# When the products of a state-space step are issued: the steps' waits are split in halves

## The chip, the cores and the metric

The kernel runs on one core of one Trainium2 chip. The metric is the device time of one execution in microseconds (us). Engines are called as in the profile: PE (TensorE, matrix products), PEld (its weight loads), DVE (VectorE), ACT (ScalarE), POOL (GpSimd), SP (SyncE, which here starts DMAs).

## The reference

Two layers of a hybrid backbone on 256 context tokens and 256 latent tokens, width 2048, in float32. Each layer normalizes and modulates the tokens, multiplies them by one large input weight, feeds three mixers side by side (a gated linear recurrence "LRU" in both directions, windowed attention, and a state-space mixer "SSD" in both directions), and multiplies their outputs by one large output weight. The part around the change is the chunked state-space sum:

```python
    Acs = jnp.cumsum(dt * A.reshape(G, R), axis=2)
    ...
    decay = jnp.exp(jnp.where(tril, seg, -jnp.inf))
    CB = jnp.einsum('bcign,bcjgn->bcijg', Cm, Bm)
    Wm = CB[..., None] * decay * dt[:, :, None]
    y_diag = jnp.einsum('bcijgr,bcjgrp->bcigrp', Wm, x)
    w_state = jnp.exp(A_last[:, :, None] - Acs) * dt
    states = jnp.einsum('bcjgn,bcjgrp->bcgrpn', Bm, x * w_state[..., None])
    ...
    y_off = jnp.einsum('bcign,bcgrpn->bcigrp', Cm, h_in) * jnp.exp(Acs)[..., None]
    y = (y_diag + y_off).reshape(bsz, L, SSD_HEADS, SSD_HEAD_DIM)
```

The sequence is cut into chunks of 128 tokens: a state per chunk, carried from chunk to chunk, and for each chunk an output from the tokens within it (`y_diag`) and from the carried state (`y_off`).

## The kernel before

The large weights go through PE in blocks of 128x128, 16 for one column tile of the input weight. A DMA brings four blocks (`raw`), ACT copies them to the rounded format (`hi`, L237), DVE subtracts to get the rest (`lo`, L238), and PE multiplies each block in three passes (hi by u, hi by the rest of u, lo by u; all through the helper's L174, as `acc<-u,hi` and `acc<-u,lo`). Three passes are called a block below. A block is 512 columns wide in layer 0, and partly 256 in layer 1, where some columns are needed for the latent tokens alone.

Between blocks the mixers' own work is issued. Each mixer is a Python generator that yields a wait; the kernel keeps a planned clock (`self.clock`) that only PE's instructions move forward, a full block by 0.647 (three times 512/2400+0.0025), and after each block `pump()` resumes those generators whose wait is over. So a wait is a number of blocks, rounded up, and PE's order is fixed in the program by these waits. The orders of DVE, ACT, POOL and SP are made from it by the language's scheduler, by its own model. None of the planned times is a measured one.

`ssd_core` is one of these generators. It goes through 28 steps in layer 0 and 20 in layer 1. A step has a beginning, its elementwise work, and an end, its products:

- State: the beginning is one DVE multiplication (`xw`, L1119). The end is the PE product `mx<-xw,Btok`, then ACT copies it to `H` (L1128), or DVE multiplies `H` by its decay (L1130) and adds the product (L1132).
- Output, written y(chunk, half) below: the beginning is, for the first half of a chunk, the PE product `mx<-CT,BT` and two masks of it (`cbm`, L1151); for each half two DMAs of broadcast rows (`bc`, L1158, four buffers) and the decays: `ee` in four columns on ACT (L1164) and DVE (L1165), `ww` in four columns on ACT (L1167) and DVE (L1168), an exponential (L1170), `ee` times `ww` (L1171), and for each carried state an exponential of `bc` (L1175) and a multiplication by CT (L1176). The end is 12 small PE products (`mx<-ee,X`, `mx<-bc,H`), or 8 where only one state is carried, and one DVE addition (L1191). The first group's chunk order is 0, 1, 3, 2, the second's too.

The LRU runs at the same time. For each of its columns it issues two "gate pairs", one per direction, a short wait ("lx2") apart: four products `mx<-xc,gw` and `mx<-xsw,gw` into two buffers, each freed by a tanh on ACT (`lt`, L712). Further ACT work (L717, L718, L720, and a square root with its table load at L724), POOL (L727) and DVE scans (L730, L733, L735) follow. State products, `mx<-CT,BT`, output products and gate pairs take turns in four PSUM buffers `mx`; three more, `acc`, hold the large products.

`self.wait("core")` is 4 in layer 0 and 5.2 in layer 1. The waits differ in blocks: 4 is 7 full blocks, 5.2 is 9 full blocks or 16 of half width. Work that waits for `core_done`: the z column tiles of a layer, which follow later in the program, and in layer 0 `ada_wide` (DMA at L377, DVE at L380), which computes later modulations.

Of the kernel before, what the change touches and what calls it, by code (L numbers as in the profile page):

```python
# [139 lines left out]
class Kernel:  # L140
# [471 lines left out]
    def ssd_core(self, l):  # L612


        yield lambda: self.ssd_ready == 13
        ends = []
        for g in range(2):
            f1, r1 = self.ssd_state(0, g, 0), self.ssd_state(1, g, 1)
            steps = [f1, r1]
            if l == 0:  # L620
                steps += [self.ssd_y(g, 0, hh, None, r1) for hh in range(2)]
                steps += [self.ssd_y(g, 1, hh, f1, None) for hh in range(2)]
            f2, r2 = self.ssd_state(0, g, 1, f1, True), self.ssd_state(1, g, 0, r1, True)
            f3, r3 = self.ssd_state(0, g, 2, f2), self.ssd_state(1, g, 3, r2, True)
            steps += [f2, r2, f3]
            steps += [self.ssd_y(g, 3, hh, f3, r2) for hh in range(2)]
            steps += [r3]
            steps += [self.ssd_y(g, 2, hh, f2, r3) for hh in range(2)]
            for step in steps:
                step.begin()  # L630
                ends.append(step)
                yield self.wait("core")
                if len(ends) > 1:
                    ends.pop(0).end()
        yield self.wait("core")
        ends.pop(0).end()
        self.core_done = True

# [638 lines left out]
```

## Time and profile before

| what | before |
|---|---|
| median of 3 executions | 1833.83 us (1833.53 to 1835.87) |
| the profiled execution | 1829.47 us |
| its span | 1827.5 us |
| mean granted clock of PE | 0.991 |
| PE busy | 1765.5 us, 97% of the span |
| DVE busy | 1407.4 us, 77% |
| ACT busy | 973.3 us, 53% |

A busy share is a mean over the whole span. The steps of `ssd_core` run from about 257 to 453 us in layer 0 and from about 1265 to 1445 us in layer 1. Windows of the profile give the busy time of each engine within such a stretch. "PEclk" is the granted clock of PE, 1.00 for full speed. The list of PE's waits says for which operation's end PE stood idle, and the timeline shows such an idle time in brackets behind the instruction that ended it.

### The profile page before, as it was taken

The numbers are of one execution on the slowest core, as the hardware profiler recorded it, in microseconds if no ns is written. First come the engines' busy times: TensorE is split into PE (matmuls) and PEld (weight loads), VectorE is DVE, ScalarE is ACT, GpSimd is POOL, SyncE is SP. The second block draws the span as 40 slices with busy tenths as digits, with TensorE's granted clock in tenths as the row PEclk, the third lists the DMA queues.
The fourth block names the chain that finished last, engine by engine and source line by source line (L and its number), as shares of the span: only waits on it lengthen the run. The fifth ranks groups of instructions, "written<-read, shape, count | busy, mean of one in ns | idle before, by whom it ended". The sixth has DMA issues, their size and how long they took to land.

```text
span 1827.5 us, 30170 instructions
## 1 busy us (share of the span) xinstructions
PE 1765.5 (97%) x10522; PEld 1453.4 (80%) x10522; DVE 1407.4 (77%) x3117; ACT 973.3 (53%) x1798; POOL 214.7 (12%) x179
## 2 busy tenths in 40 slices
PE   7999999999999999999999999999989999999999
PEld 4677876667778778887888887888767788999999
DVE  4447769898899778899999536877688785788665
ACT  4324578688523354556232235545688863678443
POOL 0000111111210021211000021010021130121000
PEclk9999999999999999999999999999999999999999
DMA  9982333434675545556766433455243564554655
GB/s 364 389 292 66 124 104 102 122 122 146 220 221 180 179 150 185 178 182 221 238 220 222 158 122 107 133 185 168 96 138 107 179 214 142 182 178 155 217 185 179
DMA packets 186344, 322.99 MB, mean 177 GB/s; under 512 B 19121, under 2 KB 44625, under 8 KB 185553
## 3 DMA queue, kind: packets, MB, share of 16 engines
q1 hardware_dynamic: 186192, 321.09, 54.2%
q8 instruction: 82, 1.34, 0.3%
q14 instruction: 70, 0.57, 0.1%
HBM read 310.38 MB, written 10.63 MB: 176 GB/s over the span
## 4 chain that ended last, share of the span: by engine, by line
PE 72%; DVE 9%; issue 7%; ACT 7%; DMA 3%; POOL 1%; SPq 0%; ACTq 0%; DVEq 0%; POOLq 0%
PE acc L174 55%; PE mx L174 13%; PE ada L174 3%; DVE lo L238 2%; PE mx L170 2%; DMA bc<-acsD 1%; ACT hi L237 1%; DVE ada L380 1%; DVE araw L380 1%; ACT lt L712 1%; DVE lh L730 1%; DMA araw<-in_adaw_dram 1%; DVE xc L466 1%; DVE ee L1165 1%; ACT ww L1167 1%
## 5 line engine op out<-in xcount | busy, mean ns | idle before, releaser
L174 PE MATMUL acc<-u,hi 128*128 128x512 f32 (+1 forms) x4800 | 1277.4, 355 | 3.9 <-ACT u L452 3.1
L174 PEld LDWEIGHTS acc<-u,hi 128*128 128x128 f32 x4800 | 837.1, 190 | 149.0 <-issue 32.6
L174 PE MATMUL acc<-u,lo 128*128 128x512 f32 (+1 forms) x2400 | 842.4, 351 | 6.9 <-DVE lo L238 6.7
L237 ACT ACTIVATE hi<-raw 128x512 fp32r<-128x512 f32 x640 | 397.8, 628 | 544.4 <-PE acc L174 420.8
L238 DVE TENSOR_TENSOR lo<-raw,hi 128x512 fp32r<-128x512 f32 x640 | 457.9, 718 | 184.6 <-ACT hi L237 172.7
L174 PEld LDWEIGHTS acc<-u,lo 128*128 128x128 f32 x2400 | 455.5, 190 | 71.9 <-DVE lo L238 11.7
L380 DVE SCALAR_TENSOR_TENSOR araw<-araw,adac 128x512 f32<-128x512 f32 x256 | 183.2, 716 | 6.9 <-DMA araw<-in_adaw_dram 4.1
L380 DVE SCALAR_TENSOR_TENSOR ada<-araw,adac 128x512 f32<-128x512 f32 x192 | 141.6, 738 | 13.0 <-DMA adac<-condD 7.0
L174 PE MATMUL mx<-u,hi 128*128 128x512 f32 (+1 forms) x320 | 99.7, 395 | 0.0
L1077 DVE SCALAR_TENSOR_TENSOR X<-acc,mod,X 128x256 f32<-128x256 f32 x144 | 65.0, 478 | 39.5 <-PE acc L174 39.4
L727 POOL TENSOR_TENSOR lt<-lt,ltl 128x512 f32<-128x512 f32 x32 | 45.5, 1443 | 326.2 <-ACT ltl L724 305.3
L868 POOL TENSOR_SCALAR prob<-prob,qrs 128x512 f32<-128x512 f32 (+1 forms) x48 | 58.2, 1227 | 214.7 <-ACT hi L237 124.7
L427 POOL TENSOR_TENSOR ssq<-ssq,sq 128x512 f32<-128x512 f32 (+1 forms) x26 | 34.1, 1312 | 308.0 <-ACT sq L423 308.0
L174 PEld LDWEIGHTS mx<-u,hi 128*128 128x128 f32 x320 | 56.6, 191 | 14.2 <-issue 4.6
L174 PE MATMUL mx<-u,lo 128*128 128x512 f32 (+1 forms) x160 | 61.0, 382 | 0.0
L511 POOL TENSOR_SCALAR X<-xs,prm 128x512 f32<-128x512 f32 (+1 forms) x16 | 15.4, 968 | 361.6 <-DVE xs L489 357.1
L174 PE MATMUL mx<-xc,gw 64*64 64x512 f32 x128 | 40.8, 619 | 8.9 <-ACT lt L712 5.9
L423 ACT ACTIVATE sq<-X 128x256 f32<-128x256 f32 (+1 forms) x44 | 18.8, 452 | 54.8 <-DVE X L654 53.1
L1165 DVE SCALAR_TENSOR_TENSOR ee<-bc,nacs,ee 128x128 f32<-128x128 f32 x96 | 35.9, 427 | 15.0 <-DMA bc<-acsD 9.6
L771 POOL TENSOR_TENSOR qw<-qw,cst 128x256 f32<-128x256 f32 x20 | 23.1, 1156 | 197.7 <-DVE rt L770 169.7
L712 ACT ACTIVATE lt<-mx,gbh 128x512 f32<-128x512 f32 x64 | 42.0, 674 | 4.1 <-PE mx L174 4.0
L1164 ACT ACTIVATE ee<-bc,nacs 128x128 f32<-128x128 f32 x96 | 30.9, 390 | 17.7 <-DMA bc<-acsD 17.7
(240 smaller groups left out, 1953.1 us busy)
## 6 DMA issues: line engine op xcount, KB each, us to landing
raw<-in_w_in_dram SPq DMA_DIRECT2D x448, 256.0 KB, 2.8
araw<-in_adaw_dram SPq DMA_DIRECT2D x256, 256.0 KB, 3.0
raw<-in_w_out_dram SPq DMA_DIRECT2D x192, 256.0 KB, 3.0
ar<-in_ada_dram SPq DMA_DIRECT2D x84, 256.0 KB, 5.4
bc<-acsD SPq DMA_DIRECT2D x48, 256.0 KB, 3.7
ar<-in_ada_dram SPq DMA_DIRECT2D x22, 512.0 KB, 6.9
adac<-condD SPq DMA_DIRECT2D x28, 256.0 KB, 4.5
gw<-in_gates_dram SPq DMA_DIRECT2D x16, 256.0 KB, 2.9
```

Of the source, the lines that this page charges most:

```text
L170: self.nc.tensor.transpose(out=out, in_=lhsT, identity=rhs)
L174: self.nc.tensor.matmul(out=out, lhsT=lhsT, rhs=rhs, start=start, stop=stop, **kw)
L237: nc.scalar.activation(out=hi, in_=part, func=AF.Copy)
L238: nc.vector.tensor_tensor(out=lo, in0=part, in1=hi.bitcast(F32), op=ALU.subtract)
L380: i = nc.vector.scalar_tensor_tensor(out=o, in0=raw, scalar=1.0, in1=row[c].rearrange("p t x -> p (t x)"), op0=ALU.mult, op1=ALU.mult, acc ...
L427: nc.gpsimd.tensor_tensor(out=self.ssq[0], in0=self.ssq[0], in1=sq, op=ALU.add)
L712: nc.scalar.activation(out=t, in_=pg[g], func=AF.Tanh, scale=0.5, bias=self.gb[:, 16 * g + 8 * d + m:16 * g + 8 * d + m + 1])
L727: nc.gpsimd.tensor_tensor(out=ti, in0=ti, in1=tl[:, d], op=ALU.mult)
L868: nc.gpsimd.tensor_scalar(out=pr[j], in0=pr[j], scalar1=rs[:, j:j + 1], scalar2=1.0, op0=ALU.mult, op1=ALU.mult)
L1077: nc.vector.scalar_tensor_tensor(out=x[:, s], in0=acc[:, s.start - w0:s.stop - w0], scalar=mod[:, 2 * KT + m, c:c + 1], in1=x[:, s], op0=A ...
L1164: nc.scalar.activation(out=e[:, j], in_=bcs[0][:, j], func=AF.Identity, bias=k.nacs[:, f:f + 1])
L1165: nc.vector.scalar_tensor_tensor(out=e[:, j], in0=bcs[1][:, j], scalar=k.nacs[:, r:r + 1], in1=e[:, j], op0=ALU.add, op1=ALU.min)
```

## The change

The wait of a step is yielded in two halves, and the end of the step before is issued between them, where it stood behind the whole wait. The wait behind the last step is halved too. No instruction is added or removed; lines behind the change are one higher.

```diff
             for step in steps:
                 step.begin()
                 ends.append(step)
-                yield self.wait("core")
+                yield self.wait("core") / 2
                 if len(ends) > 1:
                     ends.pop(0).end()
-        yield self.wait("core")
+                yield self.wait("core") / 2
+        yield self.wait("core") / 2
         ends.pop(0).end()
         self.core_done = True
```

In planned blocks of layer 0, one step now follows the next by 8 blocks, where it was 7: each half of 2 is 4 blocks of 0.647, rounded up. A product stood two waits, 14 blocks, behind its step's beginning; now it stands three halves, 12 blocks, behind it. Counted from the start of the program, the first product of the core stands at block 248 (it was 250), the last at 440 (it was 422), and the z tiles begin at 448 in both. In layer 1, where most blocks are of half width, a wait of 5.2 and two of 2.6 are 16 blocks alike, and a product stands closer to its beginning by 2.6 of the planned clock. The pieces below are places where the order changed.

On DVE, in the same layer, where the elementwise work of y(1,0) of the first group ends. Before:

```order
L1165 SCALAR_TENSOR_TENSOR ee_2891<-bc_2889,nacs_2356,ee_2891 128x128 x4
L721 SCALAR_TENSOR_TENSOR ltl_2809<-la_594_2844,ltl_2809 128x512
L1168 SCALAR_TENSOR_TENSOR ww_2892<-cbm_2885,dt_2151,ww_2892 128x128 x4
L1168 SCALAR_TENSOR_TENSOR ww_2955<-cbm_2885,dt_2151,ww_2955 128x128 x4
L1176 TENSOR_TENSOR bc_2887<-bc_2887,CT_1802 128x512
L238 TENSOR_TENSOR lo_3038<-raw_3035,hi_3037 128x512
L1191 TENSOR_TENSOR X_1805<-mx_2940,X_1805 128x2x128
L1171 TENSOR_TENSOR ee_2891<-ee_2891,ww_2892 128x512
```

And now (`lh_595` is the LRU's forward scan):

```order
L1166 SCALAR_TENSOR_TENSOR ee_2900<-bc_2898,nacs_2356,ee_2900 128x128 x4
L722 SCALAR_TENSOR_TENSOR ltl_2783<-la_594_2844,ltl_2783 128x512
...
L1177 TENSOR_TENSOR bc_2896<-bc_2896,CT_1802 128x512
L238 TENSOR_TENSOR lo_3036<-raw_3033,hi_3035 128x512
L1169 SCALAR_TENSOR_TENSOR ww_2901<-cbm_2894,dt_2151,ww_2901 128x128 x4
L1192 TENSOR_TENSOR X_1805<-mx_2940,X_1805 128x2x128
L731 SCALAR_TENSOR_TENSOR lh_595_2850<-lt_583_2790,lt_584_2792 128x512
L1131 TENSOR_TENSOR H_2768<-H_2768,dec_2358 128x512
L1169 SCALAR_TENSOR_TENSOR ww_2973<-cbm_2894,dt_2151,ww_2973 128x128
L1172 TENSOR_TENSOR ee_2900<-ee_2900,ww_2901 128x512
```

The last operation that y(1,0) needs (L1171, now L1172) stands behind the LRU's forward scan; it stood ahead of it. On ACT the four `ww` of this step have also moved behind the LRU's table load and square root.

On PE, where the LRU's two gate pairs of one column meet the core's state products (in the first group, after the output run y(1,0), y(1,1)). Before, one state product and the first gate pair, two blocks, and the second gate pair:

```order
L174 MATMUL mx_3114<-xw_3030,Btok_1803 128x512
L174 MATMUL mx_3121<-xc_2994,gw_2653 64x512
L174 MATMUL mx_3122<-xc_2994,gw_2653 64x512
...
L174 MATMUL mx_3143<-xc_2994,gw_2653 64x512
L174 MATMUL mx_3144<-xc_2994,gw_2653 64x512
```

Now, the first gate pair, the state product right behind it, one block, and the second gate pair:

```order
L174 MATMUL mx_3118<-xc_2994,gw_2653 64x512
L174 MATMUL mx_3119<-xc_2994,gw_2653 64x512
...
L174 MATMUL mx_3134<-xw_3051,Btok_1803 128x512
L174 MATMUL acc_3104<-u_467,hi_3107 128x512
...
L174 MATMUL mx_3141<-xc_2994,gw_2653 64x512
L174 MATMUL mx_3142<-xc_2994,gw_2653 64x512
```

Five uses of the four `mx` buffers lie close together in both, but the two pairs are one block apart where they were two.

On PE again, at the last gate pairs that meet a state and an output's beginning together (second group, about block 386). Before, a state product, `mx<-CT,BT`, a gate pair, two blocks, and the second gate pair:

```order
L174 MATMUL mx_4102<-xw_4024,Btok_1803 128x512
L174 MATMUL mx_4106<-CT_1802,BT_1801 128x128
L174 MATMUL mx_4141<-xc_3988,gw_3637 64x512
L174 MATMUL mx_4142<-xc_3988,gw_3637 64x512
...
L174 MATMUL mx_4163<-xc_3988,gw_3637 64x512
L174 MATMUL mx_4164<-xc_3988,gw_3637 64x512
```

Now a gate pair, two blocks, the second gate pair and a state product right behind it:

```order
L174 MATMUL mx_4098<-xc_3950,gw_3621 64x512
L174 MATMUL mx_4099<-xc_3950,gw_3621 64x512
...
L174 MATMUL mx_4122<-xc_3950,gw_3621 64x512
L174 MATMUL mx_4123<-xc_3950,gw_3621 64x512
...
L174 MATMUL mx_4149<-xw_4051,Btok_1803 128x512
```

Six buffers were asked for within two blocks there, and now it is five, with the state product last.

## Rows read from the trace of the kernel before

**Rows 1.** The page: busy time, share of the span, instructions.
```profile
PE 1765.5 (97%) x10522; PEld 1453.4 (80%) x10522; DVE 1407.4 (77%) x3117; ACT 973.3 (53%) x1798; POOL 214.7 (12%) x179
```
**Rows 2.** PE's waits: what ended them; us in total, times, longest.
```profile
PE mx L174 <- ACT lt L712: 12.7, 8, 4.1
...
PE acc L174 <- DVE lo L238: 6.7, 9, 1.6
PE mx L174 <- DVE ee L1171: 4.5, 2, 3.1
...
PE mx L174 <- DVE H L1132: 2.7, 1, 2.7
PE mx L174 <- ACT xsw L694: 2.3, 1, 2.3
...
PE mx L174 <- ACT H L1128: 0.7, 2, 0.4
```
**Rows 3.** Windows: us; PE, PEld, DVE, ACT, POOL busy; PEclk; DMA share; GB/s.
```profile
257.00:453.00 196.00, 182.61 (x980) 130.44 (x979) 170.23 (x345) 154.66 (x306) 30.45 (x22) 0.97 0.37 117
290.00:300.00 10.00, 6.86 (x30) 5.50 (x30) 10.00 (x18) 5.94 (x16) 2.55 (x2) 0.66 0.32 112
339.00:347.00 8.00, 7.17 (x42) 4.71 (x42) 6.12 (x12) 8.00 (x15) 0.00 (x0) 0.79 0.33 98
440.00:450.00 10.00, 8.87 (x49) 5.87 (x50) 9.62 (x30) 9.71 (x18) 0.00 (x0) 0.83 0.48 155
453.00:580.00 127.00, 124.94 (x560) 99.59 (x560) 117.25 (x253) 51.38 (x82) 21.23 (x14) 1.00 0.66 214
1265.00:1445.00 180.00, 170.25 (x1030) 129.44 (x1029) 144.64 (x262) 137.61 (x246) 28.75 (x25) 0.99 0.38 122
```
**Rows 4.** Timeline of PE, layer 0: start, us, instruction, idle time before it.
```profile
293.20 0.70 PE L174 MATMUL mx<-ee,X 128*64 128x128 f32 x4 [3.15 <-DVE ee L1171]
...
339.83 0.77 PE L174 MATMUL mx<-xc,gw 64*64 64x512 f32 x1 [3.06 <-ACT lt L712]
...
371.73 0.40 PE L174 MATMUL mx<-ee,X 128*64 128x128 f32 x2 [1.33 <-DVE ee L1171]
372.53 0.32 PE L174 MATMUL mx<-bc,H 128*64 128x128 f32 x1 [0.39 <-ACT H L1128]
...
410.05 0.65 PE L174 MATMUL mx<-xc,gw 64*64 64x512 f32 x2 [2.75 <-DVE H L1132]
...
441.06 1.76 PE L174 MATMUL mx<-xsw,gw 64*64 64x512 f32 x4 [2.35 <-ACT xsw L694]
```
**Rows 5.** The chain of waits: 66 blocks of full width in one piece.
```profile
849.20 44.89 PE acc L174 x198
```
**Rows 6.** Timeline around y(1,0) and y(1,1), first group, ACT, DVE and PE.
```profile
280.92 1.28 ACT L724 ACT_TABLE_LOAD   x1
...
281.44 0.68 DVE L1171 TENSOR_TENSOR ee<-ee,ww 128x512 f32<-128x512 f32 x1
...
282.21 1.15 ACT L724 ACTIVATE ltl<-ltl,epss 128x1024 f32<-128x1024 f32 x1
...
283.89 0.45 PE L174 MATMUL mx<-ee,X 128*64 128x128 f32 x4
...
286.76 1.21 DVE L730 TENSOR_TENSOR_SCAN lh<-lt,lt 128x512 f32<-128x512 f32 x1
...
292.38 0.67 DVE L1171 TENSOR_TENSOR ee<-ee,ww 128x512 f32<-128x512 f32 x1
```
**Rows 7.** Timeline of PE, layer 1, the longest wait there.
```profile
1344.11 2.07 PE L174 MATMUL mx<-xw,Btok 128*128 128x512 f32 x2 [4.12 <-ACT lt L712]
```
**Rows 8.** Timeline of DVE and PE, layer 1, the output that starts soonest.
```profile
1432.29 0.68 DVE L1176 TENSOR_TENSOR bc<-bc,CT 128x512 f32<-128x512 f32 x1
...
1433.82 0.43 PE L174 MATMUL mx<-ee,X 128*64 128x128 f32 x2
```
**Rows 9.** The tile ada: durations min/median/max in ns, first and last start.
```profile
L380 DVE SCALAR_TENSOR_TENSOR ada<-araw,adac x192: 668/692/1795, 452.9 to 1016.6; 128x512 f32<-128x512 f32 x192
```

## The prediction

> **What bounds the kernel now.** The page comes first: PE is busy for 1765.5 us, 97% of the span [rows 1], so time can only be won or lost where PE stands idle or runs slowly. The windows show where the changed steps lie. From 257 to 453 us, the core of layer 0, PE is busy for 182.61 of 196.00 us, so 13.4 us are idle, and its mean granted clock is 0.97; right behind it, 453 to 580, it is busy for 124.94 of 127.00 at 1.00 [rows 3]. The core of layer 1, 1265 to 1445, has 9.75 us idle at a clock of 0.99. DVE is the busiest neighbour in layer 0, 170.23 of 196.00 (87%); ACT has 154.66. The list of PE's waits names the releasers: the tanh that frees the LRU's `mx` buffers 12.7 us in 8 waits, the last operation of an output's `ee` 4.5 us in 2, `H` 2.7 and 0.7, `xsw` 2.3 [rows 2]. The timeline gives the places in layer 0: 3.15 us before y(1,1) of the first group, 3.06 before a gate pair, 1.33 and 0.39 before y(0,0) of the second group, 2.75 before a gate pair that waits for `H`, 2.35 inside a gate pair [rows 4]. These sum to 13.03, nearly all of the window's idle time. Other waits, such as those for `lo`, are spread over the program and the change doesn't touch them.
>
> An idle stretch can cost twice. In 290 to 300 us the granted clock was 0.66, in 339 to 347 it was 0.79, in 440 to 450 it was 0.83 [rows 3], and each holds one of the long waits. The loss is 10 x 0.34 = 3.4, 8 x 0.21 = 1.7 and 10 x 0.17 = 1.7 us. Over the whole window it is 196 x 0.03 = 5.9 (rounded in the clock's second digit), so no other stretch is left, and the waits of 2.75 and 1.33 cost nothing more than themselves. The ceiling of any gain here is all of it: 13.4 + 5.9 + 9.75 + 180 x 0.01 = 30.9 us.
>
> **The change part by part.** No instruction is added or removed. A block takes 44.89 / 66 = 0.680 us [rows 5]. In layer 0 two things happen at once: steps follow each other after 8 blocks instead of 7, so the same DVE and ACT work is spread over a longer stretch, and a product stands 12 blocks behind its beginning instead of 14, so it is 2 x 0.680 = 1.36 us closer. The words for the change (later) fit the begins, not this distance.
>
> *First output run.* Before, y(1,0) had slack: its last DVE operation ran from 281.44 for 0.68 and its products began at 283.89, so 1.77 us [rows 6]. Now the forward scan (1.21) stands before that operation on DVE, and on ACT the table load (1.28) and the square root (1.15) before its `ww`. That is 3.64 more work against a slack of 1.77: a new wait of 1.9. From below it is nothing, as the products also stand a block later; from above 3.6. y(1,1) waited 3.15; its products are two blocks later, and if DVE's queue, not the beginning, sets its readiness, 3.15 - 1.36 = 1.8 remain. Bounds: 0, and 3.15 + 1.36 = 4.5. I take 1.9 + 1.8 = 3.7, so +0.55. The stretch at a low clock cost 3.4. Two waits of under 2 us are nearer to the 1.33 and 0.39, which have no such stretch beside them, than to the 3.15; but they come close together. I take half, 1.7 saved, between 0 and 3.4. Net -1.1.
>
> *The gate pairs after it.* The second pair now comes one block after the first with a state product between. Five buffers are asked for in a short time while the first pair's tanh must run. Before, there was no wait here. The nearest row is the mean of the tanh waits, 12.7 / 8 = 1.6 [rows 2]. Bounds 0 and 4.1. I take +1.6.
>
> *The gate pair at 339.83.* The same pair still meets the same output run; its two old buffers come free by the same ACT work. I take 3.06 unchanged, between 1.6 and 4.1.
>
> *y(0,0) of the second group.* Its beginning and its products are closer together, but DVE has more room before it. I take 1.33 + 0.39 unchanged; bounds 0 and 1.36 more.
>
> *The gate pairs at 410.* A state and an output's beginning no longer stand before the first pair; a state stands after the second. The wait for `H` (2.75) goes, and one tanh wait of 1.6 replaces it for the state product: -1.2. Bounds -2.75 and +1.4 (a wait of 4.1).
>
> *The gate pair at 441.06* waits for `xsw`, which is LRU work alone and keeps its place: 0.
>
> *Layer 1.* The pace stays at 16 blocks of half width, and the products come closer by 2.6 of the planned clock. The output with least slack was ready at 1432.29 + 0.68 and began at 1433.82, slack 0.85 [rows 8]. The gate pairs meet state products at nearly the same places, the longest wait being 4.12 [rows 7]. I take 0, between -1.6 and +1.6 (one tanh wait) and the slack's 2.6 - 0.85 = 1.75 above it.
>
> *What is late next.* The core ends 18 blocks, about 12.3 us, later, but still 8 blocks before the z tiles. `ada_wide` starts later by as much: its layer-0 part ran from 452.9 to 1016.6 on the tile `ada` [rows 9], and 1016.6 + 12.3 = 1029 lies 236 us ahead of layer 1's core at 1265 [rows 3], with layer 0's output projection and layer 1's first column tiles between. The z tiles' DVE and ACT work now meets `ada` from the start less: nothing either way, as PE was busy 124.94 of 127.00 there. If this cover were gone, the price would be at most those 12.3 us.
>
> The sum: -1.1 + 1.6 - 1.2 = -0.7. The profiled execution took 1829.47 (span 1827.5), so it would take 1828.8; it lay 4.36 below the median of the runs, 1833.83, and against that median the forecast is 1833.1. The bounds of the terms don't fall together; a third of them in one direction gives some 5 us.
>
> A rule weighs in here. The Trainium skill, "Perfetto Trace Analysis", section "Optimization Strategy", says that consistent bubbles, the same gap repeating on the engine that should be saturated, can mean there isn't enough SBUF or PSUM for the next tile to be allocated. The trace agrees as far as 8 waits of PE for the tanh that frees its `mx` buffers go, 12.7 us in all. By that rule the change can only move these waits, since it leaves the number of buffers as it is, and the sum would be 0 and the time 1833.8.
>
> **The rivals.**
>
> *Faster: the longer pace relieves DVE and ACT.* If the waits come from a backlog on DVE (87% busy, and 10.00 of 10.00 in 290 to 300 [rows 3]), spreading the steps by 8 / 7 makes each product's operands ready earlier relative to PE. Were half of the idle time and of the clock's loss of layer 0 to go, (13.4 + 5.9) / 2 = 9.65, the time would be 1824.2. Against it: three of the six waits [rows 4] are those of gate pairs, whose LRU work isn't spread.
>
> *Slower: products too close to their beginnings.* If an output's readiness follows its own beginning (the DMA of `bc`, the masks, ACT and DVE in turn), the outputs without slack, y(1,1) of the first group, y(0,0) of the second, and y(1,0), which now loses its slack, each wait 1.36 us more: +4.1. One more stretch at a low clock like that at 339 costs 1.7, and layer 1's closest output loses 1.75 - together +7.5, 1841.3. It decides if the first output run waits over 4.5 us in all. For it speaks that those outputs had no slack before; against it, that DVE was busy without a gap around 292.38 [rows 3, 6], so a queue and not the beginning was late.
>
> *No effect beyond a shuffle.* The distance changes by two blocks of 14, most outputs have more slack than that, and the waits for the four `mx` buffers [rows 2], gone at one place, come back at another: 1833.8. It is also what the rule of the Trainium skill above would give.
>
> **How the numbers follow.** About 0.2%, 3.7 us, is what a measurement of this kernel can tell from no change. My sum, with 0.25, and the shuffle without effect, with 0.21, both lie within it: 0.46 together. The relief of DVE has 0.28, the closeness 0.26. So faster 0.28, within 0.2% 0.46, slower 0.26. The likeliest time is 1833.1; the likeliest case's own range is 1830 to 1837. The range must leave out 2 in 10 at most: it reaches down to the relief's 1824 and up to the closeness' 1841.5.
>
> **What the profile of after would show.** Right: PE's waits in layer 0's core sum to about 12 to 14 us; a wait before y(1,0) where there was none; two shorter waits where the 3.15 stood, with a granted clock in those 10 us above 0.66; a new tanh wait just behind them; no wait for `H` of 2.75; `ada` starting at about 465. The relief would show as waits of PE that sum to about 7 us in that stretch and a clock of 0.98 or more; the closeness as waits for L1172 that sum to over 7 us. The forecast is wrong if the scheduler's new orders on DVE and ACT put `lo` or `hi` of the large blocks behind the core's work, so that waits for `lo` (6.7 us now) grow, or if the later `ada_wide` meets something that I take as covered.

## The result, and the profile after

The changed kernel is slower: a median of 1850.92 us (1847.81 to 1851.85, 4 runs) against 1833.68, a ratio of 1.0107 (95% interval 1.0088 to 1.0127), so 17 us by the medians and 20 by the ratio. The forecast was 1833.1 with a range up to 1841.5.

The profiled execution took 1851.85 us (span 1850.0), 22.4 more than that of before. The one of before lies 4.2 below its median, so what is read below from two traces is in sum some 5 us more than the medians' difference. The page of the changed kernel, then its list of PE's waits (us in total, times, longest):

```profile
PE 1776.1 (96%) x10522; PEld 1459.5 (79%) x10522; DVE 1408.4 (76%) x3117; ACT 976.0 (53%) x1798; POOL 221.8 (12%) x179
```

```profile
PE acc L174 <- DVE lo L238: 12.8, 8, 3.1
PE mx L174 <- DVE ee L1172: 11.9, 4, 4.0
PE mx L174 <- ACT lt L713: 11.8, 3, 7.8
...
PE mx L174 <- DVE X L1192: 5.2, 1, 5.2
...
PE mx L174 <- DVE xw L1120: 2.9, 1, 2.9
```

Beside [rows 1, 2]: the instructions are the same in number, and DVE and ACT do the same work, but the waits for `ee` went from 4.5 to 11.9, those for `lo` from 6.7 to 12.8, and PE now waits for an output's addition (X), which frees a buffer, and for the states' `xw`, for which it didn't wait. The tanh waits are 11.8 in 3 where they were 12.7 in 8: fewer and longer.

Windows of the changed kernel (columns as in [rows 3]), and the same stretches of before:

```profile
257.00:470.00 213.00, 192.27 (x997) 137.50 (x996) 170.34 (x336) 157.78 (x312) 33.31 (x24) 0.94 0.34 110
...
1265.00:1475.00 210.00, 192.03 (x1127) 145.91 (x1126) 155.60 (x278) 154.05 (x266) 33.64 (x26) 0.95 0.36 119
337.00:347.00 10.00, 5.62 (x17) 2.96 (x18) 7.30 (x19) 9.89 (x23) 0.00 (x0) 0.66 0.45 133
397.00:407.00 10.00, 8.20 (x37) 6.73 (x38) 9.04 (x18) 3.70 (x8) 1.10 (x1) 0.66 0.50 158
595.00:615.00 20.00, 19.44 (x102) 16.25 (x101) 18.78 (x51) 6.07 (x11) 1.15 (x1) 1.00 0.69 226
```

```profile
257.00:470.00 213.00, 199.61 (x1055) 144.50 (x1054) 186.97 (x374) 161.31 (x316) 36.42 (x26) 0.97 0.41 132
470.00:720.00 250.00, 240.47 (x1132) 195.36 (x1131) 215.96 (x523) 103.79 (x184) 35.47 (x27) 0.99 0.59 184
1265.00:1475.00 210.00, 198.68 (x1243) 153.58 (x1242) 166.14 (x297) 163.60 (x287) 35.17 (x29) 0.99 0.42 135
...
595.00:615.00 20.00, 16.66 (x75) 13.90 (x74) 17.08 (x43) 5.79 (x11) 1.18 (x1) 0.91 0.63 189
```

Half of the loss is idle time, half is the clock. With the same instructions PE's busy time rose by 10.6 us (1765.5 to 1776.1), and its idle time, the span less the busy time, by 11.9. In layer 0's core PE is idle for 20.7 us instead of 13.4, and at 0.94 instead of 0.97 it loses 213 x 0.03 = 6.4 more. In layer 1's the idle time is 18.0 instead of 11.3, and 0.95 instead of 0.99 costs 8.4 more. Together that is more than the whole, since a low clock costs nothing while PE is idle, and since part of layer 0's loss comes back behind its core. DVE's busy time in 257 to 470 fell from 187 to 170: it isn't short of time, it waits too.

Where the time was lost is seen best by blocks, since PE does the same blocks in the same order: the start of the same block's last pass in the two traces, after minus before.

```
block               240   300   400   440   500   720   1000  1500  1560  1600  1725  2500
after - before, us  -0.3  -0.9   1.7   9.7  14.2   6.5   8.0   9.1  13.3  16.1  21.8  22.5
```

Layer 0's core ends at block 440, and 14 are lost by block 500. Some 6 to 8 come back by 720: behind the later core two waits of before are nearly gone, with the lower clock at the first (0.91 in 595 to 615). They are, in before:

```profile
602.99 2.00 PE L174 MATMUL mx<-cst,rs 128*128 128x128 f32 x8 [3.34 <-DVE rs L409]
...
655.40 0.44 PE L170 MATMUL mx<-cst,prob 128*128 128x128 f32 x2 [2.86 <-POOL prob L868]
```

Layer 1's core, blocks 1509 to 1710, loses 12.7 more (between 1500 and 1725) and gives nothing back.

The timeline of PE in the changed kernel, the long waits of layer 0's core and of the blocks behind it:

```profile
287.15 0.45 PE L174 MATMUL mx<-ee,X 128*64 128x128 f32 x4 [2.74 <-DVE ee L1172]
297.20 0.45 PE L174 MATMUL mx<-ee,X 128*64 128x128 f32 x4 [1.72 <-DVE ee L1172]
...
341.38 1.12 PE L174 MATMUL mx<-xc,gw 64*64 64x512 f32 x2 [5.25 <-DVE X L1192]
398.80 0.70 PE L174 MATMUL mx<-ee,X 128*64 128x128 f32 x4 [4.00 <-DVE ee L1172]
437.24 0.43 PE L174 MATMUL mx<-ee,X 128*64 128x128 f32 x2 [3.42 <-DVE ee L1172]
451.77 1.00 PE L174 MATMUL mx<-xc,gw 64*64 64x512 f32 x1 [2.86 <-ACT lt L713]
505.04 0.50 PE L174 MATMUL acc<-u,lo 128*128 128x512 f32 x1 [2.91 <-DVE lo L238]
```

And layer 1:

```profile
1316.33 2.04 PE L174 MATMUL mx<-xw,Btok 128*128 128x512 f32 x2 [2.86 <-DVE xw L1120]
1360.11 2.07 PE L174 MATMUL mx<-xw,Btok 128*128 128x512 f32 x2 [7.78 <-ACT lt L713]
...
1424.08 0.50 PE L174 MATMUL acc<-u,lo 128*128 128x512 f32 x1 [1.62 <-DVE lo L238]
...
1453.97 0.79 PE L174 MATMUL acc<-u,lo 128*128 128x512 f32 x1 [3.09 <-DVE lo L238]
```

The 7.78 answers to [rows 7]. What caused it is read from the other engines of the changed kernel: POOL, SP's queue and ACT.

```profile
1348.69 1.06 POOL L750 TENSOR_TENSOR lh<-lh,lgt 128x256 f32<-128x256 f32 x1
...
1349.78 0.33 SPq L751 DMA_DIRECT2D lruD<-lh  x1
1350.15 0.42 SPq L685 DMA_DIRECT2D gw<-in_gates_dram  x1
1350.68 0.87 SPq L1159 DMA_DIRECT2D bc<-acsD  x2
...
1354.83 1.28 ACT L1165 ACTIVATE ee<-bc,nacs 128x128 f32<-128x128 f32 x4 [7.55 <-DMA bc<-acsD]
...
1356.53 2.43 ACT L1168 ACTIVATE ww<-cbm,dt 128x128 f32<-128x128 f32 x8
...
1359.39 0.67 ACT L713 ACTIVATE lt<-mx,gbh 128x512 f32<-128x512 f32 x1
```

The two transfers of `bc` stand on SP behind the store of the LRU's column, which waits for POOL until 1349.75. They land by 1354.8, where ACT goes on. ACT stands idle for 7.55 us at the `ee` that needs them, and the tanh that PE's buffers wait for stands behind that `ee`, and behind eight `ww`, four for each half of the chunk. The same place on ACT in before:

```profile
1338.69 2.44 ACT L1167 ACTIVATE ww<-cbm,dt 128x128 f32<-128x128 f32 x8 [1.97 <-DVE cbm L1151]
1341.67 1.29 ACT L1164 ACTIVATE ee<-bc,nacs 128x128 f32<-128x128 f32 x4 [0.54 <-DMA bc<-acsD]
...
1343.39 1.24 ACT L712 ACTIVATE lt<-mx,gbh 128x512 f32<-128x512 f32 x2
```

The eight `ww` came ahead of the wait for the transfers and filled it; the tanh ran 1.7 us after the transfers had landed. Now it runs 4.6 us after. The `ww` need the masks of `mx<-CT,BT`, which belong to the beginning that moved back.

### The profile page after: what moved, and what is told of

Its sections match the earlier page's. It is cut to its first block, busy times and chain, and to the rows that moved or that the text cites. A ratio compares the mean times of both kernels' runs of the same rounds, so it can differ in the third digit from the quotient of the medians.

```text
span 1850.0 us, 30188 instructions
## 1 busy us (share of the span) xinstructions
PE 1776.1 (96%) x10522; PEld 1459.5 (79%) x10522; DVE 1408.4 (76%) x3117; ACT 976.0 (53%) x1798; POOL 221.8 (12%) x179
## 4 chain that ended last, share of the span: by engine, by line
PE 75%; DVE 9%; issue 6%; ACT 6%; DMA 4%; POOL 1%; SPq 0%; DVEq 0%; ACTq 0%; POOLq 0%
PE acc L174 58%; PE mx L174 13%; PE ada L174 2%; DVE lo L238 2%; DMA bc<-acsD 2%; PE mx L170 2%; DVE ww L1169 1%; DVE araw L380 1%; DVE ada L380 1%; ACT lt L713 1%; ACT hi L237 1%; DMA araw<-in_adaw_dram 1%; ACT ww L1168 1%; DVE xc L466 1%; ACT lt L719 1%
## 5 line engine op out<-in xcount | busy, mean ns | idle before, releaser
L174 PE MATMUL acc<-u,lo 128*128 128x512 f32 (+1 forms) x2400 | 846.3, 353 | 13.0 <-DVE lo L238 12.8
L380 DVE SCALAR_TENSOR_TENSOR ada<-araw,adac 128x512 f32<-128x512 f32 x192 | 139.8, 728 | 11.4 <-DMA araw<-in_adaw_dram 10.3
L1166 DVE SCALAR_TENSOR_TENSOR ee<-bc,nacs,ee 128x128 f32<-128x128 f32 x96 | 31.0, 375 | 30.4 <-ACT ee L1165 15.9
L174 PE MATMUL mx<-ee,X 128*64 128x128 f32 x192 | 30.4, 298 | 13.0 <-DVE ee L1172 11.9
```

The source lines that it names most:

```text
L174: self.nc.tensor.matmul(out=out, lhsT=lhsT, rhs=rhs, start=start, stop=stop, **kw)
L380: i = nc.vector.scalar_tensor_tensor(out=o, in0=raw, scalar=1.0, in1=row[c].rearrange("p t x -> p (t x)"), op0=ALU.mult, op1=ALU.mult, acc ...
L1166: nc.vector.scalar_tensor_tensor(out=e[:, j], in0=bcs[1][:, j], scalar=k.nacs[:, r:r + 1], in1=e[:, j], op0=ALU.add, op1=ALU.min)
```

## The experiments

The kernels with "early" beginnings (e6, e7, e9, e10, e12) are the changed kernel. The others are the kernel before; e1 to e5 and e8 have this loop, where A and B are set per layer, and e11 and e13 to e18 alter it as their own pieces show. Before is A = 4, B = 0 in layer 0 and A = 5.2, B = 0 in layer 1:

```diff
                 step.begin()
                 ends.append(step)
-                yield self.wait("core")
+                yield CORE[l][0]          # A
                 if len(ends) > 1:
                     ends.pop(0).end()
+                if CORE[l][1]:
+                    yield CORE[l][1]      # B
-        yield self.wait("core")
+        yield CORE[l][0]
         ends.pop(0).end()
```

The pace is A + B, and a product stands A + B + A behind its beginning. Ratios are to the kernel before on the same chip, with 95% intervals.

### Which layer: e1, e2

```diff
+CORE = ((2, 2), (5.2, 0))        # e1_layer0
+CORE = ((4, 0), (2.6, 2.6))      # e2_layer1
```

> The split waits in layer 0 alone (2 and 2), layer 1 as before (5.2 in one piece). By block number the changed kernel fell behind by 14 us in the core of layer 0 and got 6 back before layer 0 ended, and by another 13.5 in the core of layer 1. If the two losses are independent, this one is +6 to +9 us over the kernel before, and the outputs' waits for ee in layer 0's core stay at about 12 us. If layer 1's loss came from a state that layer 0 left behind (ada later), it is +17 or more.

> The split waits in layer 1 alone (2.6 and 2.6), layer 0 as before. Independent losses: +11 to +14 us. Here the pace is the same 16 half-width blocks, so a loss of that size can't come from the pace; it is the products' nearness to their beginnings, or an accident of order. If layer 1's loss depended on layer 0, within 4 us of before.

Measured: e1 1.0034 (1.0017 to 1.0050), e2 1.0064 (1.0043 to 1.0085). The two add up to 1.0098, which lies in the interval of the whole change (1.0088 to 1.0127): the layers' losses are independent within what the runs can tell, 6 us and 12 us. Layer 1 loses the more.

One statement on layer 1 in the section on the change needs a correction. Its blocks there are not mostly of half width: counted in the traces, pieces of 16 blocks of full width and 16 of half width take turns. In a full-width piece two waits of 2.6 are 10 blocks where 5.2 is 9, so the pace isn't quite the same. Of the 20 products the first stands 4 blocks earlier than in before (1509, it was 1513), the 8th to the 13th stand at the same blocks, and the last are 1 to 4 blocks later.

### Pace or distance: e3, e4, e5, e8

```diff
+CORE = ((3.6, 1.2), (5.2, 0))    # e3: layer 0, pace 8 blocks, distance 14
+CORE = ((3.0, 1.2), (5.2, 0))    # e4: layer 0, pace 7, distance 12
+CORE = ((4.6, 0), (5.2, 0))      # e5: layer 0, pace 8, distance 16
+CORE = ((4, 0), (3.9, 1.3))      # e8: layer 1, distance 1.75 paces
```

> Layer 0 alone, one step per 8 blocks as in the changed kernel, but products 14 blocks behind their beginnings as before (waits 3.6 and 1.2). Closeness theory: the waits for ee fall from 12 to under 6 us and the time is within 4 us of before, or a little faster. Pace theory (the core's longer stretch collides with the gates): +6 to +9 as with both.

> Layer 0 alone, one step per 7 blocks as before, products 12 blocks behind (waits 3.0 and 1.2). Closeness theory: +6 to +9 us, waits for ee 8 us or more in layer 0's core. Pace theory: within 4 us of before.

> Layer 0 alone: a step per 8 blocks, the products 16 blocks behind their beginnings (one wait of 4.6). With e1 (lag 12) and e3 (lag 14) the third point at one pace. Closeness theory: no slower than lag 14, within 4 us of before or up to 8 us faster, waits for ee in layer 0's core under 5 us. If a longer pace has a price of its own, it is slower than before by 4 or more.

> Layer 1 alone, the same pace, products 1.75 paces behind their beginnings (3.9 and 1.3) where before has 2 and the change 1.5. If nearness is what costs, the loss lies between 0 and the 12 us of e2, 3 to 9. If e2's loss is one accident of order (the gate pair and the states at its begin), it is either all there or gone.

Measured: e3 0.9998 (0.9988 to 1.0008), e4 1.0055 (1.0040 to 1.0070), e5 0.9993 (0.9978 to 1.0008), e8 1.0019 (1.0008 to 1.0031). So in layer 0 the longer pace alone costs nothing in the whole, and it looked as if the distance were all of it. It wasn't: these kernels also move the products on PE, and the next ones show that this counts.

### Which part of a beginning: e6, e7, e9, e10, e12

All five are the changed kernel in both layers, with a part of each beginning issued half a pace earlier, right behind the end of the step before it.

```diff
                 if len(ends) > 1:
                     ends.pop(0).end()
+                if i + 1 < len(steps):
+                    steps[i + 1].early()
                 yield self.wait("core") / 2
```

`early` holds: in e6 the product `mx<-CT,BT` and its masks; in e7 the DMAs of `bc` and the eight `ee`; in e9 all of an output's beginning; in e10 the states' `xw`; in e12 the beginnings of both. PE's order is the same in e6, e9 and e12, and the changed kernel's own in e7 and e10.

> The changed kernel in both layers, but the product of CT and BT and its two masks are issued half a pace earlier, right behind the products of the step before, where the kernel before had them. If the nearness that costs time is that of this product, the only part of an output's beginning on PE, the loss of 17 us falls to under 6. If it is the place of the rest of the beginning in DVE's and ACT's queues, the loss stays above 12.

> The other half: the changed kernel, with the DMAs of bc and the eight ee operations of each output issued half a pace earlier, and CT by BT, its masks and ww left where the change put them. Queue theory: the loss falls to under 6 us. Theory of the product on PE: it stays above 12.

> The changed kernel with the whole beginning of each output half a pace earlier, and the states' multiplications left where the change put them. PE's order is the same, instruction for instruction, as in e6, so a difference to e6 can only come from the orders of DVE, ACT and SP. Queue theory (the rest of the beginning comes too late in DVE's and ACT's queues): the loss falls from 13.5 to under 6 us. Theory of PE's order (collisions in the four mx buffers): it stays at 10 to 16.

> The changed kernel with only the states' multiplications (xw) half a pace earlier; PE's order is that of the changed kernel. Only the wait of 2.9 us for xw in layer 1 can go by itself: a loss of 12 to 17 us of 17. If the states set the chain in both layers, under 6.

> The changed kernel with every beginning half a pace earlier (outputs and states), so that products stand where the change put them, 16 blocks behind their beginnings in layer 0 and two paces in layer 1. PE's order is again that of e6. Closeness theory: within 4 us of before, 13 us or more faster than the changed kernel. Theory of PE's order: as e6, 10 to 16 above before.

Measured: e6 1.0072 (1.0048 to 1.0096), e7 1.0081 (1.0057 to 1.0104), e9 1.0087 (1.0072 to 1.0103), e10 1.0069 (1.0053 to 1.0086), e12 1.0075 (1.0060 to 1.0090). None gives the whole loss back, not even e12, where each beginning (but the very first) is as far from its product as in e5 and, in layer 1, as in before. My theory that the distance is all of it fell here. A part comes back: by their medians e6, e10 and e12 are 13.5 to 13.9 us above before, e7 and e9 15.6 and 15.7, the change 17.2. Only e10's interval lies wholly under that of the change. With PE's order the same (e6, e9, e12), three orders of DVE, ACT and SP took the same time within their intervals. The waits only changed their names; PE's timeline of e6, layer 0:

```profile
435.26 0.32 PE L174 MATMUL mx<-bc,H 128*64 128x128 f32 x1 [3.10 <-DVE H L1140]
451.44 1.69 PE L174 MATMUL mx<-xc,gw 64*64 64x512 f32 x2 [6.90 <-ACT lt L717]
```

At the output that waited 3.42 for `ee` in the changed kernel, `ee` is now in time and `H` is late by 3.10, and at the gate pair behind it the tanh wait has grown from 2.86 to 6.90.

e10 shows what the chain of layer 1 is worth. Its products and its outputs' beginnings stand at the blocks of the changed kernel, only `xw` is earlier, but the scheduler has put the two transfers of `bc` ahead of the LRU's store on SP. SP and ACT at the place of the wait of 7.78:

```profile
1347.35 1.15 SPq L1166 DMA_DIRECT2D bc<-acsD  x2
...
1353.65 0.32 SPq L755 DMA_DIRECT2D lruD<-lh  x1
```

```profile
1350.57 1.28 ACT L1172 ACTIVATE ee<-bc,nacs 128x128 f32<-128x128 f32 x4 [0.62 <-DMA bc<-acsD]
```

ACT waits for 0.62 us instead of 7.55, the tanh follows at 1352.80, and PE has no wait at that place. By blocks, e10 loses 8.3 us between 1500 and 1725 where the change loses 12.7, so the chain is worth some 4 us of layer 1's loss. DVE's and ACT's orders differ as well, so this is support for the chain and not a test of it alone.

### Place against distance: e13 to e16

The first product of the changed kernel comes 1.5 waits behind the core's start, in before 2 waits. By "place" I mean the blocks at which the core's products stand among the LRU's gate pairs. Against e5, which has the same pace and whole waits, the split puts layer 0's products 3 to 8 blocks earlier, while the gate pairs stay within two blocks. Place and distance are set apart here, one layer at a time, with the other layer as before. e13 and e14: products where the change put them (in e14 the last four 1 or 2 blocks later), distance 2 paces. e15 and e16: the split waits with one more half wait ahead of the first step, distance 1.5. That puts the products where e5 has them, within one block, in layer 0; in layer 1 it puts them 1 to 10 blocks behind before's.

```diff
+CORE = (2, 5.2)                  # e13; e14 is (4, 2.6) with l == 1
-                yield self.wait("core")
+                yield CORE[l]
+                if l == 0 and len(ends) > 1:
+                    yield CORE[l]
...
+        if DELAY[l]:              # e15: CORE ((2, 2), (5.2, 0)), DELAY (2, 0)
+            yield DELAY[l]        # e16: CORE ((4, 0), (2.6, 2.6)), DELAY (0, 2.6)
```

> Layer 0 alone: PE's products stand where the change put them (the first half a pace earlier than in e5), but 16 blocks behind their beginnings. Theory of place (where on PE the products meet the LRU's gate pairs): +5 to +10 us over before, though the beginnings are farther than in before. Closeness theory: within 4 us of before, as e5.

> Layer 1 alone, the same: the products where the change put them, half a pace earlier than before, and two paces behind their beginnings as before. Theory of place: +5 to +12 us. Closeness theory: within 3 us of before.

> Layer 0 alone, the split waits of the change with one more half wait (2) ahead of the first step: products where e5 has them, 12 blocks behind their beginnings as in the change. Theory of place: within 4 us of before. Closeness theory: +5 to +10 us, waits for ee above 8 us.

> Layer 1 alone, the split waits with one more half wait (2.6) ahead of the first step: products where before has them, 1.5 paces behind their beginnings. Theory of place: within 4 us of before. Closeness theory: +8 to +13 us.

| | distance 2 paces | distance 1.5 paces |
|---|---|---|
| layer 0, pace 8, late place | e5 0.9993 (0.9978 to 1.0008) | e15 0.9996 (0.9980 to 1.0012) |
| layer 0, pace 8, early place | e13 1.0036 (1.0021 to 1.0050) | e1 1.0034 (1.0017 to 1.0050) |
| layer 1, place of before (e16: 1 to 10 blocks later) | before 1 | e16 1.0080 (1.0049 to 1.0111) |
| layer 1, place of the change | e14 1.0028 (1.0011 to 1.0045) | e2 1.0064 (1.0043 to 1.0085) |

In layer 0 it is the place, at either distance 6 us, and the distance is nothing. In layer 1 the one clean pair is e14 and e2, with products at the same blocks but for the last four: there the shorter distance costs 7 us (the two intervals together leave 2 to 12). In e16 distance and place changed together, 15 us. And e14 loses 5 us at the distance of before, though none of its products stands more than 6 blocks from before's. So of layer 1's 12 us some 7 are distance by these runs, and the rest is what e14 has too, with beginnings and products a few blocks from before's. The sum of e13 and e14, 1.0064, lies in the interval of e12 (1.0060 to 1.0090), which is both together.

Windows of e13 (early place) and then e15 (late place), both layer 0:

```profile
257.00:470.00 213.00, 193.05 (x995) 137.31 (x994) 171.67 (x341) 158.67 (x311) 32.97 (x22) 0.95 0.37 110
470.00:720.00 250.00, 242.66 (x1154) 197.92 (x1153) 217.75 (x519) 103.37 (x182) 38.87 (x29) 0.99 0.62 190
```

```profile
257.00:470.00 213.00, 191.57 (x1001) 138.07 (x1001) 168.78 (x335) 159.88 (x313) 38.50 (x25) 0.95 0.36 108
470.00:720.00 250.00, 248.24 (x1192) 202.65 (x1190) 222.82 (x540) 105.70 (x188) 38.51 (x28) 0.99 0.64 197
```

PE is as idle in the one core as in the other, 20.0 and 21.4 us, at the same clock. The difference lies behind the core: 7.3 us idle in 470 to 720 against 1.8. Before has 9.5 there. Counted by blocks against before, from block 100 on, e13 has lost 10.3 us at block 440 and 16.1 at 500, e15 7.8 and 9.5. Between blocks 600 and 640 both get some 5 back, as e1, e3 and e5 do and no kernel with layer 0's old pace (e4, e17, e18); the wait for `rs` stands there in before. So the core of 8 blocks' pace costs time at both places; at the late place nearly all of it comes back behind it (0.8 is left at block 720), at the early place PE's waits for `lo` eat a part (8.9 is left). PE's timeline of e13, behind the core:

```profile
498.99 0.50 PE L175 MATMUL acc<-u,lo 128*128 128x512 f32 x1 [0.92 <-DVE lo L239]
507.81 0.50 PE L175 MATMUL acc<-u,lo 128*128 128x512 f32 x1 [3.06 <-DVE lo L239]
516.06 0.50 PE L175 MATMUL acc<-u,lo 128*128 128x512 f32 x1 [0.88 <-DVE lo L239]
```

e15 has one such wait of 0.55 in their place.

In layer 1 the distance seems to show in ACT's waits. The rows are of before, the changed kernel, e14 (place of the change, 2 paces) and e16 (behind before's place, 1.5 paces), ACT's waits for the DMA of `bc` from 1265 to 1475 (us in total, times, longest):

```profile
ACT ee L1164 <- DMA bc<-acsD: 4.4, 2, 3.8
```

```profile
ACT ee L1165 <- DMA bc<-acsD: 8.6, 3, 7.6
```

```profile
ACT ee L1169 <- DMA bc<-acsD: 3.5, 1, 3.5
```

```profile
ACT ee L1170 <- DMA bc<-acsD: 16.7, 5, 5.2
```

In these four they are long at 1.5 paces and short at 2. The distance doesn't set them by itself, though: they are 3.9 in 3 in e10 at 1.5 paces, 11.1 in 3 in e8 at 1.75 and 8.3 in 3 in e11 at 2.25. What else stands in ACT's queue pays: in e16 it is also the copy `hi` of the large blocks, for which PE waits 11.1 us in 4 waits. Its timelines of PE and ACT:

```profile
1357.45 0.80 PE L175 MATMUL acc<-u,hi 128*128 128x256 f32 x2 [6.04 <-ACT hi L238]
```

```profile
1348.62 1.28 ACT L1170 ACTIVATE ee<-bc,nacs 128x128 f32<-128x128 f32 x4 [4.58 <-DMA bc<-acsD]
...
1356.77 1.14 ACT L238 ACTIVATE hi<-raw 128x512 fp32r<-128x512 f32 x2
```

### Around the optimum: e11, e17, e18

e11 gives layer 1 a distance of 2.25 paces (a step's end is issued when three have begun: A = 1.3, B = 3.9). e17 keeps e4's places in layer 0 and begins each step two blocks earlier. e18 delays before's core in layer 0 by two blocks.

```diff
-                if len(ends) > 1:
+                if len(ends) > DEEP[l]:   # e11: CORE ((4, 0), (1.3, 3.9)), DEEP (1, 2)
...
+                if l == 0 and len(ends) > 1:   # e17
+                    yield 1.2
+                yield 3.0 if l == 0 else self.wait("core")
...
+        if l == 0:                # e18, ahead of the first step
+            yield 1.2
```

> Layer 1 alone, same pace, products 2.25 paces behind their beginnings, the next point after 1.5 (+12), 1.75 (+4) and 2 (before). Closeness theory: no slower than before, 0 to 6 us faster. If 2 is an optimum of the accident of order, 4 or more slower.

> Layer 0 alone, a step per 7 blocks: every product stands exactly where e4 has it, every beginning two blocks earlier than in e4, so 14 blocks apart as before. Theory of place: +6 to +10 us like e4. Closeness theory (at pace 7): within 4 us of before.

> Layer 0 alone, the steps of before (7 blocks, 14 behind), the whole core begun two blocks later. A place two blocks off may cost or give several us: theory of place leaves -6 to +8 open; closeness theory expects within 4 us of before.

Measured: e11 1.0009 (0.9999 to 1.0019), e17 1.0022 (1.0010 to 1.0034), e18 0.9992 (0.9977 to 1.0007). e4's 10 us are thus 4 for its places and 6 for the distance: at the pace of 7 blocks the distance counts in layer 0 too. The places of e17 are within 4 blocks of before's and cost 4 us, those of e18 within 3 and cost nothing, so how far a core was moved doesn't tell what it costs. A core two blocks later, or products farther off, bring nothing that the measurement can tell. None of the kernels beats the one before.

## Why the prediction was wrong

Two terms of the sum failed: layer 1, taken as 0, lost 12 us (e2), and layer 0, summed to -0.7, lost 6 (e1). The step that failed most is layer 1's, 0 with at most 1.75 above its tanh wait. I had looked at the slack of the outputs' last operation [rows 8], and in the changed kernel no output of layer 1 waited for its `ee`. What came late was the DMA of `bc`, at the start of an output's work, and what stood behind it on ACT was other work: the tanh for which PE then waited 7.78. The slack of an operand says nothing on the work that is queued behind it. That the pace of layer 1 stays as it is was a misreading too: in the pieces of full width it is 10 blocks instead of 9.

**The first output run.** The forecast waits, 1.9 and 1.8, were 2.74 and 1.72, for the operation and the reason given. The clock, taken at half of its loss, was right too: it was 0.83 in 284 to 294, a loss of 1.7. By block 300 the changed kernel was 0.6 us ahead of where it stood at 240; the term was -1.1.

**The gate pairs after it.** The wait of 1.6 there didn't come. It came at the next pair: 5.25 instead of 3.06 [rows 4], for an output's addition (X), with a clock of 0.66 in 337 to 347 where before has 0.79 in 339 to 347 [rows 3]. I took 3.06 as unchanged.

**The gate pairs at 410** didn't wait any longer, as said, and the 1.6 taken for the state product behind them didn't come. But three new waits stand between 398 and 452, 4.00, 3.42 and 2.86, and the first has a stretch at 0.66 of its own. I summed the waits that I knew, and priced none for the outputs that had slack. y(1,0) of the second group lost its slack as y(1,0) of the first did, which I had worked out for the first group and didn't carry over.

**The later core** was not covered on both sides. I priced the stretch behind it at nothing; it first took waits for `lo` (2.91 in the changed kernel, 4.86 in e13) and then gave 6 to 8 us back. I had named a growth of the waits for `lo` as what would make the forecast wrong; they doubled.

**The slower rival** had the right sign, a price of 7.5, and the test of its mechanism came out mixed (the first output run over 4.5 us: 4.46, just missed; waits for L1172 over 7: 11.9). A loss by distance shows in layer 1 (e2 against e14), though not through an output's own wait as the rival had it, and at the pace of 7 (e4 against e17). It doesn't in layer 0 of the changed kernel, where at the pace of 8 the distance is worth nothing (e13, e15) and the place is worth 6 us. That the products move against the LRU I had noted ("block 248 (it was 250)"), but I priced it only at the few gate pairs that I listed.

**The faster rival** fell: the longer pace at 16 blocks' distance (e5) is worth 0.07%, inside the interval. DVE's busy share did fall, 187 to 170 us of 213, and that was no relief, since PE's waits were for the order on DVE and ACT and not for DVE's time.

**The rule of the Trainium skill** from "Perfetto Trace Analysis" on too few buffers isn't borne out as I used it. By it the time would have stayed at 1833.8. The count of waits for the tanh fell from 8 to 3 and their sum stayed (12.7 and 11.8), but the longest came behind ACT's wait for a DMA, so there the buffers were held by a late engine. Whether more buffers would help was not tried.

What is shown: the two layers' losses, which add up, the place in layer 0, and a loss by distance in layer 1 at one place. What is read from the traces: the chain from POOL through SP's queue and ACT to PE in layer 1, which e10 supports, and the `ww` that no longer fill ACT's wait. It was not tried to move the store or `bc` to another queue. Why the early place makes `lo` late behind layer 0's core stays open, and so does why e14, a few blocks from before, loses 5 us.

## What to carry to other kernels

A wait inside a software pipeline sets three things at once: the pace, the distance between a step's two halves, and the phase of the whole pipeline against everything else that shares its engines and buffers. Change them one at a time; here a half pace of phase was worth 6 us in layer 0 and a half pace of distance some 7 in layer 1, and a longer pace alone nothing, since what it cost came back behind the core. Count the blocks in the trace to see that only one of them changed: in layer 1 the rounding of waits moved the products as well.

When a DMA, an engine's queue and a buffer form a chain, look at what is queued behind the operation that will wait, on every engine of the chain, and not at the slack of the operation itself. And count the clock with each long wait of PE: here it was half of the loss.

## What the runs showed of the hardware

A wait on one engine was paid on another through the order of its queue, as the trace of the changed kernel shows it: ACT idle 7.55 us for a transfer, and PE idle 7.78 us for a tanh behind it that needed nothing of that transfer. The transfer itself was issued 5.8 us after the last products that read its buffer (they ended at 1344.9), behind a store on the same queue. With the transfer ahead of the store (e10), ACT's wait was 0.62 us.

PE's granted clock was 0.66 in the 10 us in which each of the waits of 5.25 and 4.00 of layer 0 ends, and 1.00 in 397 to 407 of before, where PE had no wait. In the wait of 4.00 it was still 1.00 in 394.8 to 396.5, with PE idle, and 0.50, the lower of its two levels (1.2 of 2.4 GHz), in 398 to 403, behind it. Before, the longest wait there, 3.15, had 0.66 beside it too [rows 3, 4]. So each of these three came with up to 3.4 us more by the clock, 1.6 to 2.1 times its own length in all. Not every wait did: around those of 2.75 and 1.33 of before the clock was 1.00 (406 to 414 and 365 to 380).
